# The last four expert blocks of a PEER decoder step held and multiplied by token groups, and its row gathers issued at other rates

## The chip, the cores and the metric

One core of one Trainium2 chip runs the whole program. The metric is the device time of one execution in microseconds (us). Before the change it is 3731.05 us, the median of 3 runs (3728.86 to 3739.23).

## The reference

One step of two trunk layers on 512 prompt tokens and 64 sample tokens (8 sequences of 8), 1024 channels, all in float32. Each layer has a mixer (a projection to six groups of 1024 columns, a gated linear recurrence beside a gated short convolution, an output projection) and behind it a PEER channel mixer, which is what the change touches. Cut to that:

```python
q = (xb @ w_q).reshape(tb, 8, 2, 128)
s = einsum('thpd,hpkd->thpk', q, sub_keys)
sv, si = top_k(s, 16)
fv, fi = top_k(sv[:, :, 0, :, None] + sv[:, :, 1, None, :], 16)
g = softmax(fv)
act = gelu(einsum('thkd,td->thk', u_tab[idx], xb))
out = einsum('thk,thkd->td', g * act, v_tab[idx])
```

Each of 8 heads picks 16 of 16384 experts for a token. An expert has a row of `u_tab` and a row of `v_tab`, 1024 floats each.

## The kernel before, in words

**Two ways to the same sum.** 384 prompt tokens (`TD`, three groups of 128, `NT`) take the dense way: all 16384 experts, as 128 blocks of 128, are multiplied with the tokens on TensorE, and a gate matrix that is zero for experts not chosen weighs the result. The other 128 prompt tokens (two groups of 64, `NG`) and the 64 sample tokens take the gathered way: class `Gathered` fetches, for 64 tokens with 2 halves of heads on the 128 partitions, one row of `u_tab` per partition by an indirect DMA on GpSimd (`rows_of`, L660). VectorE takes the dot product with the token (`udot`, L666), and for `v_tab` adds the weighted row to a sum (`vsum`, L682). A gather lands in one of 5 buffers of the tag `rows` and is 128 rows of 4 KB. `finish` (L734, L737) brings a group's sum to the residual x through 16 small matmuls.

**The pump.** Gathers are not issued where they arise; they are tasks in a queue (`gtasks`). `pump(n)` adds n to a credit, and for each whole credit it takes one task and traces its instructions behind the last split of a weight block (`anchor`). So the constants set how many gathers lie beside which work: `MPUMP` (2.5) per projection in the mixer, once the samples' own chain is through (that is after 18 projections in layer 0 and 16 in layer 1); `QRATE` (0) in the queries; `ARATE` (0.3) times a tick, in dense_slots (17.4 per token group) and in phase A (0.6 per product of a gate piece, 192 of them); `BPUMP` in phase B: 3.0 per block for the 56 blocks whose activations are formed there, 1.0 for the 72 blocks behind them. A layer has 389 tasks: 130 for the samples (64 dots, one weighing, 64 weighted rows, one finish) and 259 for the two prompt groups.

**The order of a layer.** `mixer_in` runs 8 channels of 6 projections (pj, L150) with `beside` called behind each of them; `mixer` then multiplies by w_out (po). `queries` forms the scores and their top 16; `dense_slots` makes the slots for the dense tokens; `phase_a` forms activations of u blocks (pu, L713) and writes the gate pieces to DRAM; `phase_b` multiplies with the v blocks (pvo, L1016).

**Phase B.** Six PSUM banks hold the output sums, two for each token group (`pv[t][q]`, the third group in the two banks of the tag u), from the first block to the last. For a block, ScalarE and VectorE split the loaded 128x1024 of `v_tab` in hi and lo (`split_blk`, L132, L133; 6 buffers of raw rows, 4 of hi and lo each), VectorE multiplies the activations by the gates (L1045), and ScalarE and VectorE split that product in two halves of the space of h2h and h2l behind the third token group (wh, wl; L1047, L1048; two blocks at a time). `products` then issues 6 matmuls of 512 columns for each of the three token groups. In the first 56 blocks the u products of a block stand between these (`meet`); in the last 56 the activations are loaded back from DRAM, and the gates are always loaded, 24 pieces per 8 blocks.

**Behind the loop** the queue is emptied (`pump(1)` a thousand times), then for each token group the two banks are evicted (ys, L1059), eight transposes (L1065) and eight scaled additions to x (L1068) follow, and squares for the next normalisation (`all_squares`, L222, summed by VectorE at L224 or by TensorE at L237). `rstd` (L237, L241, L242) takes a bank of the tag u for its sums; the next mixer's `norm_mod`, or in layer 1 the final scaling (L1102) and the stores (L1105), come behind it.

**What sets the order.** The framework's planner orders the instructions of each engine ahead of the run, by its own model of their times and by the order of the program; `high_priority` moves a piece up by so many places. On the chip each engine keeps that order.

Of the kernel before, what the change touches and what calls it, by code (L numbers as in the profile page):

```python
# [21 lines left out]
P = 128  # L22
L = 2
D = 1024
KT = D // P
# [8 lines left out]
TD = 384  # L34
NT = TD // P
# [26 lines left out]
XTS = 3  # L62
WORK = 9
SIDE = (3.0, 3.5)
MPUMP, QRATE, ARATE, BPUMP = 2.5, 0.0, 0.3, (3.0, 1.0)


O_BADA, O_N1, O_N2, O_CAB, O_RBA, O_RBX, O_LAM, O_CAW, O_CBW, NV = 0, 48, 56, 64, 72, 80, 88, 96, 128, 152
# [3 lines left out]
def hybrid_step(ctx: ExitStack, tc: tile.TileContext, xT, cT, wada, vecs, fnorm, win, wout, wq, swin, swout, swq, subk,  # L72
# [12 lines left out]
    def small(name):  # L85
        return ps.tile([P, 512], F32, tag="small", bufs=2, name=name)
# [40 lines left out]
    def split_blk(raw, nm):  # L127

        hi = st.tile([P, D], F32R, tag="hi", bufs=HIS, name=f"hi_{nm}")
        lo = st.tile([P, D], F32R, tag="lo", bufs=HIS, name=f"lo_{nm}")  # L130
        with tc.high_priority(offset=AHEAD):
            S.activation(hi, raw, AF.Copy)  # L132
            anchor[0] = V.tensor_tensor(out=lo, in0=raw, in1=hi.bitcast(F32), op=ALU.subtract).ins  # L133
        return hi, lo

    def load_pair(src, nm, ahead=AHEAD):

        raw = [st.tile([P, D], F32, tag="raw", bufs=RAWS, name=f"raw{u}_{nm}") for u in range(2)]
        with tc.high_priority(offset=ahead):
            for u in range(2):  # L140
                SY.dma_start(raw[u], src[:, u, :])
        return raw
# [14 lines left out]
    def pump(n):  # L157

        credit[0] += n
        while credit[0] >= 1.0 and gtasks:  # L160
            with tc.issue_after(anchor[0]):
                gtasks.popleft()()
            credit[0] -= 1.0
        credit[0] = min(credit[0], 1.0)
# [5 lines left out]
    def ada(l, chunks, pool=None):  # L170


        if l not in mods:
            mods[l] = cp.tile([P, 48, NSEQ], F32, tag="mod", bufs=2, name=f"mod{l}")
        for ch in chunks:
            if pool and ch >= 3:
                both = pool.tile([P, 2, D], F32, tag="both", bufs=BOTH, name=f"both{l}_{ch}")
                with tc.high_priority(offset=EARLY):
                    SY.dma_start(both, wada[l, ch])
                raw = [both[:, 0, :], both[:, 1, :]]  # L180
            else:
                raw = load_pair(wada[l, ch], f"ada{l}_{ch}", EARLY if pool else AHEAD)
            pm = small(f"pm{l}_{ch}")
            for k in range(KT):
                j = k % 4
                PE.matmul(pm[j * 32:(j + 1) * 32, 0:256], c32[:, k, :], raw[k // 4][:, j * 256:(j + 1) * 256],  # L186
                          start=(k < 4), stop=(k >= 4))
            if pool:
                S.activation(first[:, ch * 256:(ch + 1) * 256], pm[:, 0:256], AF.Copy)
                continue  # L190
            ms = st.tile([P, 256], F32, tag="rows", bufs=ROWS, name=f"ms{l}_{ch}")
            S.activation(ms, pm[:, 0:256], AF.Copy)
            settle()
            late.append(lambda l=l, ch=ch, ms=ms: bring(l, ch, 1, ms))
# [25 lines left out]
    def all_squares(c0, n, sq):  # L220

        S.activation(sq[:, :, 0:n], x[:, :, c0:c0 + n], AF.Square)  # L222
        if c0 not in ONPE:
            V.tensor_reduce(out=ss[:, c0:c0 + n], in_=sq[:, :, 0:n].rearrange("p k t -> p t k"), axis=AX.X, op=ALU.add)  # L224
            sq = None
        sums[c0] = (n, sq)
# [107 lines left out]
    def mixer_in(l, vt, mod, mx, hnh, hnl, mgf):  # L334
# [32 lines left out]
        steps = [0.0]  # L367

        def beside():

            if todo:
                ada(l, [todo.pop(0)])
            steps[0] += SIDE[l]
            while steps[0] >= 1.0:
                steps[0] -= 1.0
                if next(chain, None) is None:
                    steps[0] = -1e9
            if steps[0] < -1.0:
                pump(MPUMP)

        todo = list(range(8, 24)) if l == 0 else []
# [610 lines left out]
    def phase_b(l, pg, pc, pb, g2, gd, ad, res, u_mm, h2h, h2l):  # L992
        pv = []
        for t in range(NT):
            pv.append([(bank if t < 2 else ubank)(f"pvo{l}_{t}_{q}") for q in range(2)])

        wht, wlt = (h_[:, NT, :, :].rearrange("p k t -> p (k t)") for h_ in (h2h, h2l))
        order = list(range(NA, P, GI)) + list(range(NS_, NA, GI)) + list(range(0, NS_, GI))

        def meet(pair):  # L1000

            i0, pr = pair
            uraw = load_pair(uT[l, i0 // 2 + pr], f"ub{l}_{i0}_{pr}")
            ao = pg.tile([P, 2, TD], F32, tag="ao", bufs=2, name=f"ao{l}_{i0 + 2 * pr}")
            for u in range(2):
                i = i0 + 2 * pr + u
                hi, lo = split_blk(uraw[u], f"ub{l}_{i}")
                pu = u_mm(i, hi, lo)
                S.activation(ao[:, u, :], pu[:, 0:TD], AF.Gelu)
            return ao  # L1010

        def products(t, n, wh, wl, vh, vl):
            tk = slice(t * P, (t + 1) * P)
            for (a, b) in ((wh, vh), (wh, vl), (wl, vh)):
                for q in range(2):
                    PE.matmul(pv[t][q], a[:, tk], b[:, q * 512:(q + 1) * 512],  # L1016
                              start=(n == 0 and a is wh and b is vh), stop=(n == P - 1 and a is wl))

        pairs = [(i0, pr) for i0 in order for pr in range(GI // 2)]
        acts = {}  # L1020
        gt = at = None
        for n, (i0, pr) in enumerate(pairs):
            for p_ in pairs[n:n + 1 + UAHEAD]:
                if p_[0] >= NA and p_ not in acts:
                    acts[p_] = meet(p_)
            if n == P // 2 - SQ:

                S.activation(pb.tile([P, 1], F32, name="spare"), eps, AF.Sqrt)
            if pr == 0:
                gt = pb.tile([P, NCH, GI, 16], F32, tag="gt", bufs=2, name=f"gt{l}_{i0}")  # L1030
                for c in range(NCH):
                    SY.dma_start(gt[:, c], gd[c][:, i0:i0 + GI, :])
                at = res.get(i0)
                if i0 < NS_:
                    at = pc.tile([P, GI, TD], F32, tag="at", bufs=2, name=f"at{l}_{i0}")
                    for c in range(GI // 2):
                        SY.dma_start(at[:, 2 * c:2 * c + 2, :], ad[i0 // 2 + c])
            vraw = load_pair(vtab[l * NEXP + (i0 + 2 * pr) * P:l * NEXP + (i0 + 2 * pr + 2) * P, :]
                             .rearrange("(a j) d -> j a d", a=2), f"v{l}_{i0}_{pr}")
            for u in range(2):  # L1040
                i = i0 + 2 * pr + u
                w = acts[(i0, pr)][:, u, :] if at is None else at[:, i - i0, :]
                vh, vl = split_blk(vraw[u], f"v{l}_{i}")
                wh, wl = (w_[:, u * TD:(u + 1) * TD] for w_ in (wht, wlt))
                V.tensor_tensor(out=w.rearrange("p (n t) -> p n t", t=16), in0=w.rearrange("p (n t) -> p n t", t=16),  # L1045
                                in1=gt[:, :, i - i0, :], op=ALU.mult)
                S.activation(wh, w, AF.Copy)  # L1047
                V.tensor_tensor(out=wl, in0=w, in1=wh.bitcast(F32), op=ALU.subtract)  # L1048
                for t in range(NT):
                    products(t, 2 * n + u, wh, wl, vh, vl)  # L1050
                pump(BPUMP[i0 < NA])
        for _ in range(1000):
            pump(1)
        ys, sq = (pb.tile([P, NT, KT, P], F32, tag="gt", bufs=2, name=f"{n_}{l}") for n_ in ("ys", "sq"))
        all_squares(TD, P, sq[:, 1])
        for t in range(NT):
            yt = ys[:, t].rearrange("p k t -> p (k t)")
            for q in range(2):
                S.activation(yt[:, q * 512:(q + 1) * 512], pv[t][q], AF.Copy)  # L1059
            cols = slice(t * P, (t + 1) * P)  # L1060
            for q in range(2):
                pt = small(f"pyt{l}_{t}_{q}")
                for kk in range(4):
                    k = 4 * q + kk
                    PE.transpose(pt[:, kk * P:(kk + 1) * P], yt[:, k * P:(k + 1) * P], ident)  # L1065
                for kk in range(4):
                    k = 4 * q + kk
                    V.scalar_tensor_tensor(out=x[:, k, cols], in0=pt[:, kk * P:(kk + 1) * P],  # L1068
                                           scalar=g2[:, k, 0:1], in1=x[:, k, cols], op0=ALU.mult, op1=ALU.add)
            all_squares(t * P, P, sq[:, 2 if t else 0])  # L1070
# [113 lines left out]
```

## Time and profile before

| | |
|---|---|
| median of 3 runs | 3731.05 us (3728.86 to 3739.23) |
| the profiled execution | 3730.17 us, span 3728.4 us |
| TensorE busy | 3501.1 us, 94% of the span, mean granted clock 0.960 |
| VectorE busy | 2961.9 us, 79% |
| GpSimd busy | 1119.1 us, 30% |
| DMA | 1032.70 MB, mean 277 GB/s |
| phase B's products, layer 0 and 1 | 1132 to 1876 us, 2945 to 3679 us |

A window's row gives the busy time of each engine in a stretch of the span, the granted TensorE clock as a share of 2.4 GHz, the mean busy share of the 16 DMA engines and what they moved. A timeline's row gives the start, the length, the instructions and, in square brackets, how long the engine stood idle ahead of it and what ended that. Busy times of GpSimd are rough.

### The profile page before, as it was taken

The numbers are of one execution on the slowest core, as the hardware profiler recorded it, in microseconds if no ns is written. First come the engines' busy times: TensorE is split into PE (matmuls) and PEld (weight loads), VectorE is DVE, ScalarE is ACT, GpSimd is POOL, SyncE is SP. The second block draws the span as 40 slices with busy tenths as digits, with TensorE's granted clock in tenths as the row PEclk, the third lists the DMA queues.
The fourth block names the chain that finished last, engine by engine and source line by source line (L and its number), as shares of the span: only waits on it lengthen the run. The fifth ranks groups of instructions, "written<-read, shape, count | busy, mean of one in ns | idle before, by whom it ended". The sixth has DMA issues, their size and how long they took to land.

```text
span 3728.4 us, 52710 instructions
## 1 busy us (share of the span) xinstructions
PE 3501.1 (94%) x18606; PEld 2910.8 (78%) x18606; DVE 2961.9 (79%) x6160; ACT 1481.8 (40%) x2027; POOL 1119.1 (30%) x830
## 2 busy tenths in 40 slices
PE   7999989989999999999959999899999999999996
PEld 4447768977789999988844576789987999998885
DVE  5338889998758888888873489899998788888887
ACT  3324343435553333333323344434456433333332
POOL 0001530052004444432320036200720355554422
PEclk9999989989999999999979999999987999999998
DMA  8775853479879999999856669524984899999994
GB/s 296 269 253 202 303 201 111 157 267 348 325 272 322 342 340 339 336 366 347 323 186 231 247 214 332 173 89 173 336 310 187 289 347 338 343 337 363 357 336 169
DMA packets 393449, 1032.70 MB, mean 277 GB/s; under 512 B 54240, under 2 KB 159840, under 8 KB 386400
## 3 DMA queue, kind: packets, MB, share of 16 engines
q1 hardware_dynamic: 267616, 554.28, 42.6%
q0 software_dynamic: 110592, 402.70, 29.8%
q10 hardware_dynamic: 14976, 72.36, 4.8%
q8 instruction: 146, 2.39, 0.2%
q14 instruction: 119, 0.97, 0.1%
HBM read 954.01 MB, written 75.15 MB: 276 GB/s over the span
## 4 chain that ended last, share of the span: by engine, by line
PE 59%; issue 17%; POOL 11%; DVE 6%; DMA 5%; ACT 2%; POOLq 0%; SPq 0%; ACTq 0%; DVEq 0%
PE pu L713 22%; PE pvo L1016 14%; PE pj L150 8%; PE pq L871 5%; POOL vrp L660 4%; POOL urp L660 4%; POOL urs L660 3%; PE po L150 2%; PE pgm L955 1%; DMA raw_wi<-in_win_dram 1%; DVE A L950 1%; DVE oh L945 1%; PE pm L186 1%; DMA vrp<-in_vtab_dram,gidx 1%; DMA raw_ada<-in_wada_dram 1%
## 5 line engine op out<-in xcount | busy, mean ns | idle before, releaser
L660 POOL DMA_INDIRECT urp<-in_utab_dram,gidx x256 | 370.8, 1448 | 558.1 <-DVE dot L666 435.2
L660 POOL DMA_INDIRECT vrp<-in_vtab_dram,gidx x256 | 352.5, 1377 | 491.9 <-DVE accp L682 457.6
L1016 PE MATMUL pvo<-hi_v,h2h 128*128 128x512 f32 x1536 | 485.4, 390 | 0.0
L1016 PE MATMUL pvo<-lo_v,h2h 128*128 128x512 f32 x1536 | 476.8, 389 | 0.0
L1016 PE MATMUL pvo<-hi_v,h2l 128*128 128x512 f32 x1536 | 461.7, 389 | 0.0
L660 POOL DMA_INDIRECT vrs<-in_vtab_dram,gidxs x128 | 217.8, 1702 | 789.1 <-DVE fid L786 373.4
L713 PE MATMUL pu<-h2h,hi_u 128*128 128x384 f32 x1152 | 397.7, 345 | 4.8 <-ACT hi_u L132 3.3
L713 PE MATMUL pu<-h2h,lo_u 128*128 128x384 f32 x1152 | 395.2, 343 | 2.3 <-DVE lo_u L133 2.3
L713 PE MATMUL pu<-h2l,hi_u 128*128 128x384 f32 x1152 | 395.7, 343 | 0.0
L660 POOL DMA_INDIRECT urs<-in_utab_dram,gidxs x128 | 171.8, 1342 | 670.2 <-issue 314.3
L133 DVE TENSOR_TENSOR lo_v<-raw_v,hi_v 128x1024 fp32r<-128x1024 f32 x256 | 312.9, 1222 | 54.9 <-ACT hi_v L132 48.0
L150 PE MATMUL pj<-hnh,hi_wi 128*128 128x512 f32 (+1 forms) x800 | 320.7, 402 | 33.2 <-ACT hi_wi L132 12.8
L1016 PEld LDWEIGHTS pvo<-lo_v,h2h 128*128 128x128 f32 x1536 | 288.3, 188 | 60.8
L1016 PEld LDWEIGHTS pvo<-hi_v,h2l 128*128 128x128 f32 x1536 | 288.3, 188 | 60.5
L682 DVE SCALAR_TENSOR_TENSOR accp<-vrp,dot,accp 128x1024 f32<-128x1024 f32 x252 | 322.7, 1280 | 12.0 <-DMA vrp<-in_vtab_dram,gidx 10.8
L1016 PEld LDWEIGHTS pvo<-hi_v,h2h 128*128 128x128 f32 x1536 | 287.3, 188 | 56.1
L150 PE MATMUL pj<-hnl,hi_wi 128*128 128x512 f32 (+1 forms) x800 | 314.6, 393 | 4.2 <-DVE hnl L281 4.2
L150 PE MATMUL pj<-hnh,lo_wi 128*128 128x512 f32 (+1 forms) x800 | 316.3, 396 | 1.9 <-DVE lo_wi L133 1.8
L666 DVE CUSTOM_DVE_ANT_0 urp<-urp,xt 128x1024 f32<-128x1024 f32 x256 | 306.0, 1219 | 1.7 <-DMA urp<-in_utab_dram,gidx 1.6
L713 PE MATMUL pu<-h2h,lo_ub 128*128 128x384 f32 x896 | 300.1, 335 | 0.0
L713 PE MATMUL pu<-h2h,hi_ub 128*128 128x384 f32 x896 | 299.9, 335 | 0.0
L713 PE MATMUL pu<-h2l,hi_ub 128*128 128x384 f32 x896 | 299.7, 334 | 0.0
(439 smaller groups left out, 7178.4 us busy)
## 6 DMA issues: line engine op xcount, KB each, us to landing
raw_v<-in_vtab_dram SPq DMA_DIRECT2D x256, 512.0 KB
raw_u<-in_uT_dram SPq DMA_DIRECT2D x144, 512.0 KB
raw_ub<-in_uT_dram SPq DMA_DIRECT2D x112, 512.0 KB
raw_wi<-in_win_dram SPq DMA_DIRECT2D x96, 512.0 KB
gd<-stg ACTq DMA_DIRECT2D x48, 1024.0 KB
gt<-gd SPq DMA_DIRECT2D x768, 64.0 KB
raw_ada<-in_wada_dram SPq DMA_DIRECT2D x86, 512.0 KB
ad<-ao ACTq DMA_DIRECT2D x56, 384.0 KB
```

The lines of the kernel that those rows point to most:

```text
L133: anchor[0] = V.tensor_tensor(out=lo, in0=raw, in1=hi.bitcast(F32), op=ALU.subtract).ins
L150: PE.matmul(out[:, c0:c1], a[:, w], b[:, k, c0:c1], start=(k == 0 and a is hi and b is xh), stop=(k == KT - 1 and a is lo))
L186: PE.matmul(pm[j * 32:(j + 1) * 32, 0:256], c32[:, k, :], raw[k // 4][:, j * 256:(j + 1) * 256], start=(k < 4), stop=(k >= 4))
L660: G.indirect_dma_start(out=rt, out_offset=None, in_=tab, in_offset=bass.IndirectOffsetOnAxis(ap=self.gidx[:, g, h, k:k + 1], axis=0))
L666: V.tensor_tensor_reduce(out=ur, in0=ur, in1=self.xt[g], scale=1.0, scalar=0.0, op0=ALU.mult, op1=ALU.add, accum_out=self.dot[:, g, h, k:k ...
L682: V.scalar_tensor_tensor(out=self.acc[g], in0=vr, scalar=w, in1=self.acc[g], op0=ALU.mult, op1=ALU.add)
L713: ends[i] = PE.matmul(pu[:, 0:TD], a[:, w], b[:, 0:NT, k, :], start=(k == 0 and a is hi and b is h2h), stop=(k == KT - 1 and a is lo)).ins
L871: PE.matmul(pqs[:, t0 * P:t1 * P], a[:, w], b[:, t0:t1, k, :], start=(k == 0 and a is hi and b is h2h), stop=(k == KT - 1 and a is lo))
L945: V.tensor_tensor(out=o, in0=iota2.unsqueeze(1).to_broadcast([P, 2, P, 2]), in1=slot(t, a, c0), op=ALU.is_equal)
L950: V.tensor_tensor(out=A[:, z], in0=oh[0], in1=slot(t, 2 + z, c0), op=ALU.mult)
L955: PE.matmul(pgm[:, n * P:(n + 1) * P], oh[1][:, n // 2, :, n % 2], A[:, z, n // 2, :, n % 2], start=(z == 0), stop=(z == 1))
L1016: PE.matmul(pv[t][q], a[:, tk], b[:, q * 512:(q + 1) * 512], start=(n == 0 and a is wh and b is vh), stop=(n == P - 1 and a is wl))
```

## The change

It has three parts. In phase B the last two pairs of blocks (four blocks) are prepared as before but not multiplied; the last pair's split products go to the space of the first token group of h2h and h2l, which no u product reads by then. Behind the loop and the emptied queue the four held blocks are multiplied for one token group, that group is evicted and added to x, and then comes the next group. In the mixer, the pump is not called in the last of the 8 channels. And the rates are changed: ARATE from 0.3 to 0.35, BPUMP from (3.0, 1.0) to (3.1, 1.4).

```diff
--- before.py
+++ after.py
@@ -62,7 +62,7 @@
 XTS = 3
 WORK = 9
 SIDE = (3.0, 3.5)
-MPUMP, QRATE, ARATE, BPUMP = 2.5, 0.0, 0.3, (3.0, 1.0)
+MPUMP, QRATE, ARATE, BPUMP = 2.5, 0.0, 0.35, (3.1, 1.4)
 
 
 O_BADA, O_N1, O_N2, O_CAB, O_RBA, O_RBX, O_LAM, O_CAW, O_CBW, NV = 0, 48, 56, 64, 72, 80, 88, 96, 128, 152
@@ -375,7 +375,7 @@
                 steps[0] -= 1.0
                 if next(chain, None) is None:
                     steps[0] = -1e9
-            if steps[0] < -1.0:
+            if steps[0] < -1.0 and c < KT - 1:
                 pump(MPUMP)
 
         todo = list(range(8, 24)) if l == 0 else []
@@ -995,6 +995,9 @@
             pv.append([(bank if t < 2 else ubank)(f"pvo{l}_{t}_{q}") for q in range(2)])
 
         wht, wlt = (h_[:, NT, :, :].rearrange("p k t -> p (k t)") for h_ in (h2h, h2l))
+
+        whe, wle = (h_[:, 0, :, :].rearrange("p k t -> p (k t)") for h_ in (h2h, h2l))
+        held = []
         order = list(range(NA, P, GI)) + list(range(NS_, NA, GI)) + list(range(0, NS_, GI))
 
         def meet(pair):
@@ -1041,19 +1044,25 @@
                 i = i0 + 2 * pr + u
                 w = acts[(i0, pr)][:, u, :] if at is None else at[:, i - i0, :]
                 vh, vl = split_blk(vraw[u], f"v{l}_{i}")
-                wh, wl = (w_[:, u * TD:(u + 1) * TD] for w_ in (wht, wlt))
+                last = n == P // 2 - 1
+                wh, wl = (w_[:, u * TD:(u + 1) * TD] for w_ in ((whe, wle) if last else (wht, wlt)))
                 V.tensor_tensor(out=w.rearrange("p (n t) -> p n t", t=16), in0=w.rearrange("p (n t) -> p n t", t=16),
                                 in1=gt[:, :, i - i0, :], op=ALU.mult)
                 S.activation(wh, w, AF.Copy)
                 V.tensor_tensor(out=wl, in0=w, in1=wh.bitcast(F32), op=ALU.subtract)
-                for t in range(NT):
-                    products(t, 2 * n + u, wh, wl, vh, vl)
+                if n >= P // 2 - 2:
+                    held.append((2 * n + u, wh, wl, vh, vl))
+                else:
+                    for t in range(NT):
+                        products(t, 2 * n + u, wh, wl, vh, vl)
                 pump(BPUMP[i0 < NA])
         for _ in range(1000):
             pump(1)
         ys, sq = (pb.tile([P, NT, KT, P], F32, tag="gt", bufs=2, name=f"{n_}{l}") for n_ in ("ys", "sq"))
         all_squares(TD, P, sq[:, 1])
         for t in range(NT):
+            for h_ in held:
+                products(t, *h_)
             yt = ys[:, t].rearrange("p k t -> p (k t)")
             for q in range(2):
                 S.activation(yt[:, q * 512:(q + 1) * 512], pv[t][q], AF.Copy)
```

## Rows read from the trace of the kernel before

**Rows 1.** The page: its span and the first row of part 1.
```profile
span 3728.4 us, 52710 instructions
...
PE 3501.1 (94%) x18606; PEld 2910.8 (78%) x18606; DVE 2961.9 (79%) x6160; ACT 1481.8 (40%) x2027; POOL 1119.1 (30%) x830
```

**Rows 2.** Windows: length, busy us by engine (instructions), granted clock, DMA share, GB/s.
```profile
1570.00:1640.00 70.00, 70.00 (x311) 57.95 (x310) 60.06 (x68) 25.84 (x34) 28.43 (x22) 1.00 0.98 351
1640.00:1840.00 200.00, 200.00 (x892) 165.92 (x891) 165.65 (x203) 74.16 (x98) 63.16 (x50) 1.00 0.95 347
1840.00:1876.00 36.00, 36.00 (x160) 29.68 (x159) 31.59 (x31) 11.24 (x15) 18.92 (x15) 1.00 0.90 314
1876.00:1906.00 30.00, 1.06 (x6) 0.81 (x5) 23.12 (x18) 0.00 (x0) 18.02 (x15) 0.55 0.82 287
...
3367.00:3437.00 70.00, 70.00 (x310) 57.95 (x310) 64.02 (x71) 26.66 (x36) 39.87 (x24) 1.00 1.00 369
3437.00:3637.00 200.00, 200.00 (x892) 165.88 (x891) 166.31 (x205) 73.76 (x97) 67.91 (x50) 1.00 0.96 348
3637.00:3679.00 42.00, 42.00 (x186) 34.57 (x185) 33.84 (x33) 11.66 (x16) 19.51 (x16) 1.00 0.63 211
3679.00:3694.00 15.00, 0.16 (x1) 0.00 (x0) 11.56 (x9) 0.00 (x0) 7.38 (x6) 0.57 0.75 259
```

**Rows 3.** Chain of waits, products of layer 1: start, us, what.
```profile
3367.15 114.28 PE pvo L1016 x504
```

**Rows 4.** Timeline, end of layer 0's products: start, us, instructions, idle before.
```profile
1875.64 0.61 PE L1016 MATMUL pvo<-hi_v,h2l 128*128 128x512 f32 x2
...
1905.19 3.68 PE L734 MATMUL pf<-eye,accp 128*128 128x64 f32 x16 [28.94 <-DVE accp L682]
...
1923.10 1.74 DVE L242 RECIPROCAL ss<-ss 128x256 f32<-128x256 f32 x1
...
1931.52 0.58 PE L150 MATMUL pj<-hnl,hi_wi 128*128 128x256 f32 x1 [3.11 <-DVE hnl L281]
```

**Rows 5.** Timeline, end of the span, and VectorE's groups from 3697 on.
```profile
3678.54 0.61 PE L1016 MATMUL pvo<-hi_v,h2l 128*128 128x512 f32 x2
...
3692.67 1.28 DVE L682 SCALAR_TENSOR_TENSOR accp<-vrp,dot,accp 128x1024 f32<-128x1024 f32 x1 [0.31 <-DMA vrp<-in_vtab_dram,gidx]
...
3700.35 3.02 ACT L1059 ACTIVATE ys<-pvo 128x512 f32<-128x512 f32 x6
...
3721.57 3.26 DVE L1102 SCALAR_TENSOR_TENSOR y<-x,fn,ss 128x256 f32<-128x256 f32 x8
...
L1102 DVE SCALAR_TENSOR_TENSOR y<-x,fn,ss 128x256 f32<-128x256 f32 (+1 forms) x24 | 8.2, 414 | 0.1
...
L1068 DVE SCALAR_TENSOR_TENSOR x<-pyt,mod,x 128x128 f32<-128x128 f32 x24 | 6.5, 340 | 0.0
...
L242 DVE RECIPROCAL ss<-ss 128x256 f32<-128x256 f32 (+1 forms) x3 | 4.0, 1350 | 1.2 <-ACT ss L241 1.2
```

**Rows 6.** VectorE's weighted rows from 1876 to 1906, and from 3679 to 3700.
```profile
L682 DVE SCALAR_TENSOR_TENSOR accp<-vrp,dot,accp 128x1024 f32<-128x1024 f32 x18 | 23.1, 1285 | 6.1 <-DMA vrp<-in_vtab_dram,gidx 5.8
...
L682 DVE SCALAR_TENSOR_TENSOR accp<-vrp,dot,accp 128x1024 f32<-128x1024 f32 x9 | 11.6, 1285 | 3.8 <-DMA vrp<-in_vtab_dram,gidx 3.6
```

**Rows 7.** The page, DMA queues: packets, MB, share; q0 carries the 768 gathers.
```profile
q0 software_dynamic: 110592, 402.70, 29.8%
```

**Rows 8.** Windows in the mixers' last channels, columns as in rows 2.
```profile
500.00:520.00 20.00, 18.27 (x79) 14.21 (x78) 20.00 (x27) 6.60 (x11) 6.67 (x6) 1.00 0.61 198
...
2340.00:2360.00 20.00, 18.60 (x71) 15.25 (x72) 20.00 (x25) 1.31 (x4) 10.57 (x6) 0.84 0.53 170
```

**Rows 9.** Windows ahead of the products, columns as in rows 2.
```profile
780.00:800.00 20.00, 10.37 (x62) 10.06 (x60) 19.30 (x35) 4.84 (x7) 15.37 (x7) 0.84 0.75 250
...
2680.00:2700.00 20.00, 20.00 (x123) 19.55 (x121) 19.76 (x26) 7.24 (x10) 11.70 (x8) 1.00 1.02 406
...
2780.00:2800.00 20.00, 16.20 (x110) 10.32 (x109) 19.52 (x55) 14.27 (x15) 0.00 (x0) 0.50 0.47 198
```


## The prediction

> **What bounds the kernel now.** The page comes first [rows 1]: the span is 3728.4 us and TensorE is busy for 94% of it, so most of the time is matmul time, and what can be won is where TensorE stands still or runs at 1.2 GHz, the lower of its two clock levels. The windows over the products (phase B) show such a place in each layer [rows 2]: TensorE is busy for every microsecond from 1570 to 1876 and from 3367 to 3679, and in the windows behind it does almost nothing (1.06 of 30 us; 0.16 of 15 us). The chain of waits gives the pace of the products: 504 matmuls in 114.28 us, 0.227 us each [rows 3]; a block is 18 of them, 4.08 us.
>
> The timeline says what that standstill is made of. In layer 0 the last product ends at 1876.25, and the next TensorE instruction, the sum over the gathered rows (L734), starts at 1905.19 after 28.94 us of waiting for VectorE's last weighted row [rows 4]. Then come evictions, transposes, residual, squares, reciprocal (1923.10) and the next layer's first full run of projections (1931.52). In layer 1 the last product ends near 3679.1 and the span ends 49.3 us later: the last gathered row is added at 3692.67, the evictions start at 3700.35 though their banks were full since 3679, and the last output scaling starts at 3721.57 [rows 5]. The cause stands in the code: the pump counts credit for gathers, and a full count gives 365 of 389 tasks issued before the flush in layer 0 and 370 in layer 1. The remaining 24 and 19 run when nothing is left to cover them; 18 and 9 of their additions fall behind the last product, at 1.28 us each [rows 6].
>
> **The credit after the change.** Mixer: six pumps of 2.5 fewer, 15 tasks fewer in each layer. Dense slots and phase A: the ticks add up to 167.4, so 50.2 tasks become 58.6. Phase B's first 56 blocks: 168 become 173.6. That puts both layers at the second part within one task of where they stand now (292.2 against 293.2 in layer 0). Its 72 blocks then issue up to 100.8 in place of 72, and all 389 are out some 3 blocks (layer 0) and 6 blocks (layer 1) before the end. The flush has nothing left.
>
> **Term 1, the end of layer 0.** The 72 held matmuls are the same 16.3 us of TensorE work, in another order. Behind group 0 its two evictions, eight transposes, residual and squares lie beside group 1's and 2's products. Moved in front of the end are 16 of the 24 transposes and the 16 matmuls of L734, about 5 us of TensorE at full clock (an estimate: L734's took 3.68 us, behind a window with a mean granted clock of 0.55 [rows 2, 4]). What cannot move is the statistics of the first 256 columns: L237's bank is one of the two that group 2's sums hold, so it waits for group 2's eviction, some 1.5 us behind the last product; 18 matmuls, a square root and its handoffs, about 3 us, bring the reciprocal to 4.5 us behind it. Now it stands at 1923.10 - 1876.25 = 46.9 us. So 46.9 - 4.5 - 5 = 37 us are won, and what follows the reciprocal stays.
>
> **Term 2, the end of layer 1.** Behind the last product VectorE has left: a third of the residual's 6.5 us, all reciprocals, 4.0, and all output scalings, 8.2 [rows 5]. That is 14.4 us, with 2.5 us of waiting for the first transposes ahead (an estimate: two of the six evictions that took 3.02 us [rows 5], 1.0 us, and more than as much again for transposes and handoffs) and 3.6 us for the last store (the end less 3721.57 + 3.26 [rows 5]); 20.5 us in place of 49.3. Less the same 5 us: 24 us.
>
> **Term 3, what the moved gathers cost in the second part.** On VectorE 0.4 more additions of 1.28 us per block, 0.5 us [rows 6]; it is busy 165.65 of 200 us there [rows 2], 3.4 of 4.08 us, and comes to 3.9. That fits: between 1840 and 1876, where 15 gathers went out in 36 us (1.7 per block), TensorE has no gap [rows 2]. The DMA fits less well. A gather is 402.70 MB / 768 = 0.524 MB [rows 7]. By the tile sizes a block loads 0.524 MB of V, 0.197 of gates and, where activations come back, 0.197 more: 1.44 MB in 4.08 us, 353 GB/s, and the windows show 347 and 348 at a busy share of 0.95 and 0.96 [rows 2]. With 1.4 gathers it is 1.65 MB, 405 GB/s. How much the queues can carry no row shows as a limit. Bounds: nothing, since 20 us at 406 GB/s occur with TensorE full [rows 9]; and the 347 GB/s of the long windows as a ceiling, 4.76 us a block, 0.68 us for each of the 56 blocks that reload, 38 us a layer. Another 70 us ran at 369 GB/s without a gap [rows 2]. I take 385, between 369 and 406: 4.29 us a block, 0.21 us over some 53 blocks, 11 us, of which the six raw and five gather buffers absorb a part: 8 us a layer, 16 in all. If the cover goes, V or a gathered row lands late, VectorE waits in order, and the products behind it are late.
>
> **Term 4, the mixer's last channel.** VectorE is full there (20.00 of 20 us at 500 and at 2340) and TensorE has gaps, and its mean granted clock at 2340 is 0.84, so it stood at 1.2 GHz for a part of that [rows 8]. Fifteen additions and dots less are 18 us of VectorE work, and 15 transfers less on loaded queues. TensorE's idle time and lost clock there bound the gain at 16 us a layer; nothing is the other bound, if the planner lets other gathers slip into that place. I take 8 a layer, a gain of 16, since the gap lies beside VectorE's work but a part is weight loading.
>
> **Term 5, more gathers before phase B.** 8.4 more a layer at 1.28 us [rows 6], 10.7 us of VectorE, where it is the bound: 19.30 of 20 at 780 with TensorE at 10.37, and 19.52 at 2780 with TensorE at a granted 0.50, the 1.2 GHz level, busy for 16.20 of 20 us [rows 9]. From 2680 to 2700 TensorE is full beside them. Between 0 and 10 us a layer; I take 6, 12 in all.
>
> The other edits (the second pair of held tiles in space that no U product still reads, the later release of four split buffers) cost nothing that I can name: the next layer's first weights are split within 4 us of the end, before its statistics are ready.
>
> **Sum:** 37 + 24 - 16 + 16 - 12 = 49 us. The profiled execution took 3730.2 us, 0.9 below the median of 3731.05; 3730.2 - 49 = 3681 us.
>
> **Rivals.** (a) *The transfers set the pace of the second part.* Place: the 112 blocks that reload, in both layers. Price: at a ceiling of 341 to 347 GB/s, the long windows' mean, 4.8 us a block, 76 us or more in all, against 65 us of terms 1, 2, 4 and 5 together. The sum turns at about 350: at 341 it is 85 us of loss and 3750 us, slower than before. For it speak shares of 0.95 to 1.00; against it 369 over 70 us [rows 2] and 406 over 20 [rows 9]. Beside this stands the Trainium skill's page "DMA: Bandwidth & Descriptors", section "Specifications": one core's share of HBM is given as about 358 GB/s. By that figure a block takes 4.61 us, and an estimate of the sum is about 3724 us. The windows at 369 and 406 do not agree with it as a ceiling. (b) *The held groups don't overlap*: the planner puts the evictions behind all products, or ScalarE waits in order behind the square of the gathered tokens, as the evictions did until 3700 [rows 5]. Then only the flush is won, 29 + 15 us, less 16, plus 4: 3698 us. (c) *Free cover*: no stall, no cost in phase A, 61 + 16 to 20 us: 3650 us. (d) *The gathers are not gone by the end*: late by a dozen, 15 us in each layer, 3711 us.
>
> **Chances.** The forecast's case 0.6 (3660 to 3703), (b) 0.09, (c) 0.13, (d) 0.06, (a) 0.12, of which 0.06 ends above the old time. A measurement of this kernel tells 0.3%, 11 us, from no change: 3720 to 3742 counts as the same. The range from 3642 (case c with a good order in the mixer) to 3714 (bad bounds of terms 3 and 5) leaves out under 2 in 10.
>
> **What would show it.** Right: no weighted row added behind the last product; evictions of group 0 at 10 us ahead of the last product; TensorE idle behind it 7 to 10 us in layer 0; a span that ends about 20 us behind it in layer 1; windows of the second part with TensorE below 200 of 200 only by some us; DMA share near 1.0 and above 360 GB/s. Wrong: the second part much over 306 and 312 us with VectorE waiting on gathered rows; a longer stretch at 0.50 in phase A; L734 still behind the products.

## The result and the profile after

The changed kernel takes 3764.35 us, the median of 4 runs (3762.59 to 3767.05), against 3733.99 us (3728.86 to 3739.23) for the kernel before on the same chip: a ratio of 1.0082, 95% interval 1.0064 to 1.0099. It is 30 us slower where 49 us less were forecast, and it lies outside the range. The span of the profiled execution is 3760.8 us, 32.4 more than before [rows 1]; TensorE's busy time is the same to 0.3 us, 3500.8.

Windows of the kernel after, with the columns of [rows 2]:

```profile
1640.00:1840.00 200.00, 200.00 (x892) 165.91 (x891) 165.90 (x204) 75.17 (x100) 65.95 (x49) 1.00 0.95 342
...
1876.00:1906.00 30.00, 0.00 (x0) 0.00 (x0) 23.41 (x19) 0.00 (x0) 22.40 (x18) 0.53 0.87 303
1906.00:1920.00 14.00, 2.78 (x13) 2.78 (x14) 9.40 (x8) 0.00 (x0) 4.70 (x4) 0.50 0.57 212
...
3699.50:3730.00 30.50, 3.26 (x16) 2.83 (x14) 21.48 (x17) 0.00 (x0) 17.79 (x14) 0.57 0.73 263
```

The first row is the surprise. With 1.4 credits per block in place of 1.0, GpSimd did 49 instructions in 200 us, 50 before [rows 2], and the transfers did not rise. The other rows show the standstill behind each layer's products, longer than before. VectorE's weighted rows, of the kernel after, from 1876 to 1921 and from 3700 to 3730, against 18 and 9 in [rows 6]:

```profile
L682 DVE SCALAR_TENSOR_TENSOR accp<-vrp,dot,accp 128x1024 f32<-128x1024 f32 x26 | 33.4, 1284 | 8.4 <-DMA vrp<-in_vtab_dram,gidx 7.9
...
L682 DVE SCALAR_TENSOR_TENSOR accp<-vrp,dot,accp 128x1024 f32<-128x1024 f32 x17 | 21.8, 1285 | 6.5 <-DMA vrp<-in_vtab_dram,gidx 6.1
```

Eight more in each layer. The timeline of the kernel after, at the ends of layer 0 and layer 1 (those of [rows 4, 5] answer to them):

```profile
1875.24 0.61 PE L1019 MATMUL pvo<-hi_v,h2l 128*128 128x512 f32 x2
...
1917.22 3.68 PE L734 MATMUL pf<-eye,accp 128*128 128x64 f32 x16 [41.37 <-DVE accp L682]
...
1922.60 1.06 ACT L222 ACTIVATE sq<-x 128x1024 f32<-128x1024 f32 x1 [48.36 <-DVE x L737]
1923.56 3.02 ACT L1068 ACTIVATE ys<-pvo 128x512 f32<-128x512 f32 x6
...
1944.91 0.58 PE L150 MATMUL pj<-hnl,hi_wi 128*128 128x256 f32 x1 [3.12 <-DVE hnl L281]
...
3699.31 0.61 PE L1019 MATMUL pvo<-hi_v,h2l 128*128 128x512 f32 x2
...
3727.17 3.68 PE L734 MATMUL pf<-eye,accp 128*128 128x64 f32 x16 [27.24 <-DVE accp L682]
```

L734 waits 41.37 us in place of 28.94 [rows 4]. All six evictions (L1068) still stand together, behind the square of the gathered tokens (L222): ScalarE waited 48.36 us for that square while the banks of the held groups were full. So the held groups overlap with nothing.

Where the 32.4 us of span came from:

| stretch | before | after | difference |
|---|---|---|---|
| start to the last product of layer 0 | 1876.25 | 1875.85 | -0.4 |
| from there to the first full run of projections of layer 1 | 55.3 | 69.1 | +13.8 |
| from there to the last product of layer 1 | 1747.6 | 1755.0 | +7.4 |
| from there to the end | 49.3 | 60.9 | +11.6 |

### The profile page after: what moved, and what is told of

Its sections match the earlier page's. It is cut to its first block, busy times and chain, and to the rows that moved or that the text cites. A ratio compares the mean times of both kernels' runs of the same rounds, so it can differ in the third digit from the quotient of the medians.

```text
span 3760.8 us, 52704 instructions
## 1 busy us (share of the span) xinstructions
PE 3500.8 (93%) x18606; PEld 2911.9 (77%) x18606; DVE 2966.8 (79%) x6160; ACT 1479.6 (39%) x2025; POOL 1078.9 (29%) x830
## 4 chain that ended last, share of the span: by engine, by line
PE 22%; issue 12%; POOL 8%; DVE 5%; DMA 2%; ACT 1%; POOLq 0%; DVEq 0%; SPq 0%; ACTq 0%
PE pu L713 9%; PE pj L150 4%; POOL vrp L660 4%; POOL urp L660 3%; PE pq L871 2%; PE po L150 1%; DVE A L950 1%; PE pvo L1019 1%; DVE oh L945 1%; POOL urs L660 1%; DMA vrp<-in_vtab_dram,gidx 1%; DMA raw_wi<-in_win_dram 1%; PE pgm L955 1%; DVE urs L666 0%; PE sa_gb L475 0%
## 5 line engine op out<-in xcount | busy, mean ns | idle before, releaser
L660 POOL DMA_INDIRECT urp<-in_utab_dram,gidx x256 | 338.2, 1321 | 534.8 <-DVE dot L666 322.1
L660 POOL DMA_INDIRECT vrp<-in_vtab_dram,gidx x256 | 343.3, 1341 | 483.4 <-DVE accp L682 443.9
L660 POOL DMA_INDIRECT vrs<-in_vtab_dram,gidxs x128 | 219.3, 1713 | 814.2 <-DVE fid L786 189.9
L660 POOL DMA_INDIRECT urs<-in_utab_dram,gidxs x128 | 171.8, 1342 | 748.3 <-issue 317.0
```

The source lines that it names most:

```text
L660: G.indirect_dma_start(out=rt, out_offset=None, in_=tab, in_offset=bass.IndirectOffsetOnAxis(ap=self.gidx[:, g, h, k:k + 1], axis=0))
```

## The experiments

The theory after the result: the products take a fixed number of gathers, set by the order on VectorE and not by the credit, so whatever leaves the mixer comes out behind the last product, where each row costs TensorE its whole time. The rivals: the held groups are what costs; the higher rates are what costs; the transfers are.

**1 and 2. The parts apart.** The held groups alone, with the rates and the mixer of before:

```diff
+                if n >= P // 2 - 2:
+                    held.append((2 * n + u, wh, wl, vh, vl))
...
+            for h_ in held:
+                products(t, *h_)
```

> The held groups alone, all rates and the mixer's pumps as before. Order theory (the instruction order that the planner writes puts the evictions of the output sums behind the square of the gathered tokens on ScalarE, so the held groups have nothing to overlap with): the same time as before, within 8 us, and the first eviction (ys) starts behind the last weighted row, as before. Rival (the held groups themselves cost, by buffers that are free later): 10 us or more slower than before. Rival (the groups overlap and the rates alone cost): 15 us or more faster than before.

Measured: 3737.31 us, ratio 1.0005 (0.9996 to 1.0015), no difference.

Then the rates and the mixer's condition alone, with nothing held:

```diff
+MPUMP, QRATE, ARATE, BPUMP = 2.5, 0.0, 0.35, (3.1, 1.4)
...
+            if steps[0] < -1.0 and c < KT - 1:
```

> The rates and the pump left out in the mixer's last channel, without the held groups. Order theory (phase B takes about one weighted row for each block whatever its credit is, so what the mixer no longer takes is added behind the last product): 25 to 35 us slower than before, 25 to 26 weighted rows behind the last split of layer 1 in place of 18, and 48 to 50 weighted rows in 200 us of the second part, as before. Rival (the loss comes from the held groups): within 10 us of before.

Measured: 3764.74 us, ratio 1.0076 (1.0059 to 1.0093). The whole loss is in the rates and the mixer, and the held groups give nothing.

**3. The square behind the evictions.** The change, with the square of the gathered tokens moved behind the loop over the token groups:

```diff
-        all_squares(TD, P, sq[:, 1])
         for t in range(NT):
...
             all_squares(t * P, P, sq[:, 2 if t else 0])
+        all_squares(TD, P, sq[:, 1])
```

> The changed kernel with the square of the gathered tokens moved behind the loop over the three token groups; the same work. Order theory: the evictions start within some us of the last product of their group, while gathers still land, and the chain behind the last gathered row shortens by 12 to 18 us in each layer: 3730 to 3742 us. Rival (the evictions wait for something else, as the banks or the tile they write): no earlier evictions, 3760 to 3768 us.

Measured: 3756.15 us, ratio 1.0053 (1.0036 to 1.007). Its timeline at the end of layer 0 (last product 1873.52):

```profile
1866.31 1.09 ACT L1067 ACTIVATE ys<-pvo 128x512 f32<-128x512 f32 x2 [3.93 <-PE pvo L1019]
...
1873.34 1.08 ACT L1067 ACTIVATE ys<-pvo 128x512 f32<-128x512 f32 x2 [1.43 <-PE pvo L1019]
...
1915.44 3.68 PE L734 MATMUL pf<-eye,accp 128*128 128x64 f32 x16 [41.92 <-DVE accp L682]
1918.91 1.06 PE L1073 MATMUL pyt<-ident,ys 128*128 128x128 f32 x4
```

The evictions now come where the forecast had them, but the transposes (L1073) stand behind L734 on TensorE, and L734 waits for the gathered rows as before. The end of layer 0 takes 68.3 us in place of 69.1, that of layer 1 57.3 in place of 60.9. So neither branch of the expectation came: the evictions moved, but the ends are not 12 to 18 us shorter.

**4. A forced order.** As 3, and VectorE's subtraction for h2l is tied behind the gather's arithmetic traced three blocks earlier (done[0] holds the latest such instruction, udot's or vsum's):

```diff
+                if len(marks) >= 3 and marks[-3] is not None:
+                    with tc.issue_after(marks[-3]):
+                        V.tensor_tensor(out=wl, in0=w, in1=wh.bitcast(F32), op=ALU.subtract)
...
+                done[0] = None
                 pump(BPUMP[i0 < NA])
+                marks.append(done[0])
```

> As the one before, and the order on VectorE is held to the credit: the low half of a block's weights is ordered behind the gathered rows that were issued three blocks earlier. The order then has 46 and 40 weighted rows in two times 28 blocks where the changed kernel has 32 and 27, and none behind the last product of layer 1. Order theory (the transfers of the chip can carry it): the products keep TensorE at 198 or more of 200 us, nothing is left behind them, 3680 to 3705 us. Rival (the transfers are full at 350 GB/s): TensorE loses 10 to 38 us in the second part of each layer, DMA share at 1.0, VectorE waits for gathered rows, 3710 to 3760 us.

Measured: 3740.0 us, ratio 1.001 (1.0001 to 1.002). No weighted row is left behind either last product. But the second parts are longer; its windows, and TensorE's waits from 1500 to 1900 (us, times, longest):

```profile
1500.00:1860.00 360.00, 337.27 (x1503) 280.39 (x1503) 310.97 (x364) 124.43 (x164) 166.71 (x119) 0.99 0.98 359
...
3360.00:3640.00 280.00, 256.86 (x1112) 209.75 (x1111) 239.31 (x277) 93.97 (x121) 127.97 (x92) 0.98 0.97 357
...
PE pvo L1021 <- DVE h2l L1056: 22.7, 13, 3.4
```

TensorE is idle for 22.7 of 360 us and for 23.1 of 280, all of it waiting for VectorE. The products of layer 0 last 778.2 us in place of 744.1: beside the idle time, some 3.5 us of the end's work now stands among them, and behind some waits the granted clock is lower (0.83 from 1710 to 1720). What the end of the layer gave, the products gave back. The time is that of the rival, but its sign is not there. VectorE's waits for transfers from 1500 to 1860 are

```profile
DVE at L1051 <- DMA at<-ad: 5.0, 2, 2.6
DVE accp L683 <- DMA vrp<-in_vtab_dram,gidx: 1.9, 3, 0.9
```

so gathered rows (accp) were hardly ever late.

**5. The mixer's condition alone.**

```diff
-            if steps[0] < -1.0:
+            if steps[0] < -1.0 and c < KT - 1:
```

> Only the condition on the mixer's last channel; the rates stay those of before and nothing is held. In the program's order 35 gathers of layer 1 stand behind the last product, 18 before. If what leaves the mixer has no place in the blocks and comes out at the end of the layer: 17 more there at about 1.65 us each in both layers is +56 us, less the mixer's 16 us of my forecast: 3770 to 3780, the last products some 16 us earlier in all and the two ends of layers some 28 us longer each. If instead the loss of the changed rates comes from the higher rates (gathers beside the attention, credit in the second part), this run is as before or a little faster: 3720 to 3735.

Measured: 3764.84 us, ratio 1.0077 (1.0063 to 1.0092). GpSimd's gathers (L660) ahead of, in and behind the products of layer 0 (columns: length, GpSimd busy and instructions, granted clock, DMA share, GB/s), first of this run:

```profile
0.00:1113.80 1113.80, 159.41 (x118) 0.96 0.70 248
1113.80:1858.00 744.20, 318.20 (x238) 1.00 0.95 340
1858.00:1940.00 82.00, 37.57 (x30) 0.57 0.60 208
```

and of the kernel before:

```profile
0.00:1132.10 1132.10, 189.52 (x131) 0.95 0.71 250
1132.10:1876.20 744.10, 314.04 (x239) 1.00 0.95 341
1876.20:1931.00 54.80, 17.82 (x15) 0.62 0.47 161
```

13 gathers fewer ahead of the products, 15 more behind them, and in the products 238 against 239. (A gather that a boundary cuts counts on both sides.) The products start 18.3 us earlier (1113.8) and L734 waits 27.4 us longer. This line alone loses as much as the whole change.

Only a part of the 18.3 us was won in the mixer. The first gate product of phase A (L955) starts 3.8 us earlier, and 14.5 us are won from there to the first product, this run first:

```profile
804.30:1113.80 309.50, 48.30 (x40) 0.97 0.91 329
...
808.10:1132.10 324.00, 48.10 (x38) 0.94 0.87 314
```

That stage has as many gathers as before, and a higher granted clock; why it is shorter stays open. In layer 1 the stretch from the first full projections to the queries is 7.4 us shorter, and the stages from there to the products are as long as before.

**6. The attention's rate alone.**

```diff
-MPUMP, QRATE, ARATE, BPUMP = 2.5, 0.0, 0.3, (3.0, 1.0)
+MPUMP, QRATE, ARATE, BPUMP = 2.5, 0.0, 0.35, (3.0, 1.0)
```

> Only the attention's rate, 0.35 for 0.3. In the program's order 10 gathers of layer 1 stand behind the last product, 18 before. If the end of the layer counts gathers: 8 fewer at about 1.65 us in both layers is -26 us, against some 12 us of my forecast for the gathers beside the attention: 3715 to 3727. If the loss of the changed rates sits in the higher rates: 3745 to 3765, with a longer time before the first product and a longer stretch at the low clock.

Measured: 3712.29 us, ratio 0.9927 (0.9912 to 0.9943), faster by 23 us. 142 gathers ahead, 237 in the products, 5 behind them. The products of layer 0 start 10.9 us later but end only 2.2 later, since 64 matmuls of other stages that stood among them now stand ahead, and L734 waits 14.93 us in place of 28.94.

**7. Held groups and the later square, rates and mixer of before.** The diffs of 1 and 3 together.

> The held groups with the square of the gathered tokens behind them, the rates and the mixer of before. If the evictions of the held groups are worth what they gave under the changed rates (8.6 us between the two runs there), 3727 and the ends of both layers some 4 us shorter each. If the held groups are only worth something where the end of the layer is long: 3734 to 3738, no difference.

Measured: 3732.51 us, ratio 0.9992 (0.9983 to 1.0), 3 us at the edge of what can be told. The end of layer 0 takes 55.1 us (55.3 before), that of layer 1 45.7 (49.3).

**8. The change turned round.** As 7, with another rate in the attention:

```diff
-MPUMP, QRATE, ARATE, BPUMP = 2.5, 0.0, 0.3, (3.0, 1.0)
+MPUMP, QRATE, ARATE, BPUMP = 2.5, 0.0, 0.4, (3.0, 1.0)
```

> The change turned round: the mixer keeps its gathers in the last channel, the attention's rate is 0.4, the credit of the blocks is that of before, and the groups are held with the square behind them. 2 gathers of layer 1 stand behind the last product in the program's order, 18 before. If the end of the layer counts gathers: 16 fewer at about 1.65 us in both layers is -53 us, the held groups -8, and the gathers beside the attention give back 12 to 25 us: 3690 to 3705, faster than both. If gathers ahead of the products cost as much as behind them, or lengthen the stretch at the low clock by what they save: 3730 to 3745.

Measured: 3711.52 us, ratio 0.9935 (0.9923 to 0.9948): faster than both, by less than was expected, and not to be told from run 6. The gathers of layer 0 (columns as in 5):

```profile
0.00:1143.10 1143.10, 205.84 (x150) 0.95 0.72 256
1143.10:1881.00 737.90, 315.57 (x234) 1.00 0.95 342
1881.00:1920.00 39.00, 0.00 (x0) 0.78 0.11 28
```

L734 waits 2.21 us, and the end of layer 0 takes 26.9 us in place of 55.3. But layer 1 needs 1776.1 us from its first full projections to its last product, 28.5 more than before.

**9 and 10. The rate by layer.** As 8 with `ARATE` (0.4, 0.35) by layer; then the same with layer 1's ticks of phase A at twice the rate in the second half of its gate pieces, and none in the first:

```diff
-            pump(ARATE[l] * us)
+            pump(ARATE[l] * us * (1.0 if l == 0 else 2.0 if ti >= 0.5 * len(tasks) else 0.0))
```

> As the change turned round (e8_opposite), with the attention's rate 0.4 in layer 0 and 0.35 in layer 1. Layer 0 as there: first full projections of layer 1 near 1930, 2 weighted rows behind the last product. Layer 1 as with the attention's rate alone: some 18 us shorter from there to its last product than in the run turned round, some 8 rows more behind that product's last gathers, 13 us dearer at most. If a gather in the stretch ahead of layer 1's low clock costs more than one behind the products: 3698 to 3706. If both cost the same: 3709 to 3714, no difference to the run turned round.

Measured: 3704.66 us, ratio 0.9918 (0.9905 to 0.9931). Layer 1's stretch is 1754.0 us, 22.1 shorter than in 8, its end 31.3 us, 7.7 longer. Where layer 1 loses in run 8 is above all the stage of the gate pieces in phase A: it is 17.3 of the 28.5 us, from the first gate product (L955) to the first product. Windows of run 8 in it, columns as in [rows 2]:

```profile
2750.00:2760.00 10.00, 5.84 (x46) 4.56 (x45) 9.93 (x20) 4.17 (x4) 2.98 (x4) 0.83 1.01 407
2760.00:2770.00 10.00, 3.32 (x24) 2.29 (x24) 9.90 (x24) 3.15 (x3) 4.70 (x5) 0.50 0.97 362
...
2780.00:2790.00 10.00, 6.70 (x47) 4.34 (x45) 9.83 (x26) 5.27 (x5) 1.88 (x2) 0.50 0.86 313
```

VectorE is full, the transfers of the first two run at a share of 0.97 to 1.01, TensorE waits (busy for 3.32 of 10 us), and its clock falls to 0.50. In the kernel before:

```profile
2760.00:2770.00 10.00, 10.00 (x83) 9.14 (x82) 9.23 (x21) 5.56 (x6) 2.15 (x2) 1.00 0.78 256
2770.00:2780.00 10.00, 6.46 (x59) 4.56 (x57) 9.86 (x26) 7.00 (x7) 0.94 (x1) 0.83 0.89 335
```

There TensorE was busy until 2770, and its clock fell some 20 us later than in run 8. Run 8 had begun the stage 17 us earlier (first gate product: 2677.9 against 2695.1), so counted from there the fall comes at nearly the same place; but the clock came back at about 2848 in both, so run 8 spends some 20 us more at the lower level.

> As e9_by_layer, but in layer 1 the attention's second phase issues its gathers in its second half only, at twice the rate. If what the gathers cost there is that VectorE has no free time ahead of the low clock (39 of 40 us busy from 2740 to 2780) but has from 2860 to 2940 (24 to 32 of 40): the stretch 2740 to 2780 keeps TensorE as busy as before (36 of 40) and the time is 5 to 10 us under e9_by_layer. If the planner puts them where it did anyway, as it did with the credit of the blocks: no difference.

Measured: 3701.77 us, ratio 0.9909 (0.9895 to 0.9923), not to be told from 9. From 2740 to 2780 TensorE is busy for 29.29 of 40 us, 28.79 in 9, with 9 gathers in both, so the gathers stayed where they were: the second branch. It and 9 are the fastest kernels of this study, 0.8 to 0.9% under the kernel before.

**11. Run 8 without the held groups.** The kernel before with the diff of 8 and nothing else.

> e8_opposite without the held groups (and without the square moved): the change's first part taken away where no weighted row stands behind the products. If the held groups are worth something only where nothing of VectorE's comes behind the last product: the two ends of layers are 10 to 25 us longer in all than in e8_opposite, 3722 to 3735. If they are worth the 3 us that they gave with the mixer of before: 3713 to 3716.

Measured: 3714.74 us, ratio 0.994 (0.9925 to 0.9954), not to be told from 8. In the traces, layer 0's end takes 26.7 us (26.9 with the held groups), layer 1's 32.1 (23.6 with them). But the products of layer 1 take 742.6 us with them and 738.2 without, since transposes and sums of the end now stand among them. So in these two traces the held groups are worth some 4 us in layer 1 and nothing in layer 0, which agrees with the 3 between the medians. One trace of a kernel has its limits: runs 8, 9, 10 and 11 issue layer 0's gathers at the same rate, and its last product ends at 1881.0, 1883.6, 1882.8 and 1891.8.

**12. The blocks' credit alone.**

```diff
-MPUMP, QRATE, ARATE, BPUMP = 2.5, 0.0, 0.3, (3.0, 1.0)
+MPUMP, QRATE, ARATE, BPUMP = 2.5, 0.0, 0.3, (3.1, 1.4)
```

> Only the credit of the blocks, (3.1, 1.4) for (3.0, 1.0). In the program's order 15 gathers of layer 1 stand behind the last product, 18 before, and layer 0's are where they were. If the credit does not decide how many gathers run beside the products: 3728 to 3737, the rows per 200 us of the second part unchanged (about 49). If it does, as my forecast had it: rows per 200 us up by a third, and 3700 to 3715.

Measured: 3730.35 us, ratio 0.9986 (0.9978 to 0.9995), the first branch. Its gathers in the products of layer 0:

```profile
1133.10:1877.20 744.10, 311.85 (x240) 1.00 0.96 342
```

240 with the higher credit, 239 without, and 18 weighted rows behind the last product in both. In layer 1 it moved a little: 242 gathers in the products for 239, 6 weighted rows behind them for 9, and an end some 5 us shorter.

**13 and 14. Whether the products have room.** As 4, with six blocks of slack; in 13 the tie stands at the product of gates and activations, the block's first step on VectorE, in 14 at h2l as in 4:

```diff
-                if len(marks) >= 3 and marks[-3] is not None:
-                    with tc.issue_after(marks[-3]):
+                if len(marks) >= 6 and marks[-6] is not None:
+                    with tc.issue_after(marks[-6]):
```

> As e4_cadence, but VectorE is tied at the first step of a block (the gates times the activations), and to the gather's arithmetic traced six blocks earlier, not at the last step (h2l) and three blocks earlier. If the products can take the gathers that left the mixer, and TensorE's 22.7 us of waiting for h2l in layer 0 came from where the tie stood: TensorE idle under 5 us in each second part, no weighted row behind the last product, 3705 to 3720. If the second part is full, of transfers or of VectorE's handoffs: TensorE idle 15 us and more in each, 3732 to 3745 as with e4_cadence.

Measured: 3751.59 us, ratio 1.0048 (1.0035 to 1.0061): the second branch by its sign, with a time above it. TensorE is idle for 22.3 of 360 us from 1500 and 17.9 of 280 from 3360, now waiting for ScalarE's h2h, which stands behind that product.

> As e4_cadence with the tie at h2l left where it was and six blocks of slack in place of three. If only the slack was short: like e13_cadence_tie_earlier, under 3720. If the place of the tie matters and not the slack: 3735 to 3745, with TensorE waiting for h2l as before.

Measured: 3735.97 us, ratio 1.0003 (0.9993 to 1.0013), the second branch. Its windows, and TensorE's waits from 1500 to 1900:

```profile
1500.00:1860.00 360.00, 341.40 (x1523) 285.31 (x1522) 306.76 (x363) 126.87 (x165) 154.97 (x114) 0.98 0.98 355
...
3360.00:3640.00 280.00, 264.85 (x1174) 218.65 (x1174) 241.97 (x281) 99.74 (x128) 124.91 (x92) 0.99 0.99 365
...
PE pvo L1021 <- DVE h2l L1056: 17.7, 8, 3.2
```

Three forced orders put 259 gathers into layer 0's products, and each left TensorE idle for 15 to 23 us in the second part of each layer. None kept TensorE fed. Were the transfers the limit? In run 14, in layer 0's 360 us, VectorE and ScalarE together waited 4.1 us for transfers (6.5 in the kernel before), while TensorE was idle for 18.6: there, late transfers are not the reason. In run 13 ScalarE waited 14.2 us for them in the same stretch, so there they may have a part.

**The runs together**, all for layer 0 but where two numbers stand (layer 0, layer 1). The kernel before was measured again beside each group of runs, with medians of 3733.99 to 3737.35 us; the ratios above are to those.

| kernel | gathers ahead, in, behind the products | weighted rows behind the last product | L734 waits, us | time, us |
|---|---|---|---|---|
| before | 131, 239, 15 | 18, 9 | 28.9, 14.9 | 3733.99 |
| after | 126, 238, 21 | 26, 17 | 41.4, 27.2 | 3764.35 |
| 5, mixer's condition | 118, 238, 30 | 34, 26 | 56.4, 43.9 | 3764.84 |
| 6, attention's rate | 142, 237, 5 | 10, 2 | 14.9, 1.6 | 3712.29 |
| 12, blocks' credit | 131, 240, 15 | 18, 6 | 28.9, 9.6 | 3730.35 |
| 8, turned round | 150, 234, 0 | 2, 0 | 2.2, 0 | 3711.52 |

The wait follows the count: from 2 to 34 rows it grows by 54.2 us, 1.69 us a row, of which 1.28 is VectorE's addition; the rest is mostly the wait for the row's own gather, as in the groups shown above (7.9 us on 26 rows).

## Why the prediction was wrong

**The step that failed** is in "The credit after the change": "Its 72 blocks then issue up to 100.8 in place of 72", and from it "The flush has nothing left". A credit was taken for a gather that runs there. Credit only traces a task; where it stands among VectorE's instructions the planner decides, and on the chip GpSimd waits for VectorE: GpSimd's waits in the kernel before, from 1500 to 1840 (us, times, longest), are:

```profile
POOL vrp L660 <- DVE accp L682: 213.5, 88, 7.7
```

A gather waits for the row that gives its buffer back. Run 12 shows how little the credit decides: by the sum it would have emptied the flush of its 24 and 19 tasks, and 1 and 3 gathers more ran in the products. What the section counted ahead of the products nearly came (126 gathers for 131, and 145 for 146 in layer 1); it was the products that did not take more, 238 for 239 and 241 for 239. Why the planner leaves the order as it is was not shown. The range could not hold the result, since no case in it had more rows behind the products than before.

**Terms 1 and 2** (37 and 24 us won) came as 13.8 and 11.6 us lost. Two steps fell. The rows behind the products rose by eight in each layer, 12.4 us of L734's wait. And "behind group 0 its two evictions, eight transposes, residual and squares lie beside group 1's and 2's products" did not happen: rival (b) had the reason right, ScalarE in order behind the square, and run 3 showed that TensorE's transposes stand behind L734 too. With both out of the way, run 8 against 11, the overlap is worth some 4 us in layer 1, where the sum had 9 (24 less the 15 of rival (b)), and nothing in layer 0, where it had 8 (37 less 29). The price of the flush was about right: emptied alone, run 11, it shortened the ends by 28.6 and 17.2 us, where rival (b) had 29 and 15. The terms failed because the change did not empty it.

**Term 3** (16 us lost) was not put to the test by the change, since no gather moved into the second part: 49 instructions of GpSimd for 50 in 200 us. The forced orders did put them there and cost 15 to 23 us of idle TensorE a layer where 8 were forecast, and mostly not in the way forecast ("V or a gathered row lands late, VectorE waits in order"): TensorE waited for VectorE's or ScalarE's splits, but VectorE waited for gathered rows only 1.9 us in run 4 and 0.8 in run 14, in layer 0's 360 us. The transfers ran at a share of 0.97 to 0.99 meanwhile; whether a better order has room stays open.

**Term 4** (16 us won, 8 a layer in the mixer's last channel) was right for layer 1: alone, run 5, 7.4 us are won there. In layer 0 it is 3.8 us, and the other 14.5 by which the products start earlier come from phase A, of which the term says nothing. **Term 5** (12 us lost): alone, run 6, layer 0's products end 2.2 us later and layer 1's stretch grows by 9.9; that the two add up to 12 is in part luck, since the term had 6 in each layer. Together in the changed kernel the two cancel in layer 0 (-0.4 for a forecast of -2) and lose 7.4 us in layer 1. They do not add: run 6 gains 23 us and run 5 loses 29, but with both, run 2, the loss is again 29. Why the attention's rate is worth nothing beside the mixer's condition was not tried further, nor was the change without that condition and with its own rates.

**The rivals.** (a) had the sign, with the wrong mechanism and place: nothing was lost beside the loads, since layer 0's products took 744.1 us in both kernels. (Those of layer 1 took 744.2 for 737.9, with 42 matmuls more from the stage ahead among them and TensorE never idle.) Of the Trainium skill's page "DMA: Bandwidth & Descriptors", section "Specifications", the 358 GB/s did not hold as a ceiling either: run 14 moved 365 GB/s over 280 us. (b) and (d) together are nearest, but (d) had a dozen rows late and set that against 18; the count went the other way.

In numbers: terms 1 and 2 missed by 86.4 us (61 won against 25.4 lost), term 3 by -16, terms 4 and 5 together by 11.0 (4 won against 7.0 lost; run 5 shows that this stretch holds more than the two terms). That makes 81.4, the 49 forecast and the 32.4 of span.

## What to carry to other kernels

A rate of issue is a wish: before counting what a stretch will take, count in the trace what it took, and ask which engine's order gives the buffers back. When work leaves one place and the place meant for it does not take more, it comes out at the end, where its full time counts: here 1.69 us a row behind the products. So price each place by a run that moves work to it alone; the one line that started layer 0's products 18 us earlier lost, by itself, as much as the whole change.

## What the runs showed of the hardware

The transfers were not at their limit at the 347 GB/s of the kernel before: with more gathers forced beside the products, the queues moved 365 GB/s for 280 us at a share of 0.99, with TensorE busy for 265 us of it. And a few more gathers in a stage where VectorE is full can cost more than their own additions, 1.28 us each: in runs 8 and 11, 10 gathers more than before stand ahead of layer 1's products, and the stretch from its first full projections to its last product is 28.5 us longer in run 8 (some 4 of it work of the layer's end) and 23.3 in run 11. TensorE waits there for VectorE, and in run 8 its clock is at 0.50, the 1.2 GHz level, for some 20 us more. In layer 0 the same rate brings 19 gathers more ahead of the products, which end 4.7 and 15.5 us later in the two runs.
